# Prompt attention's masks: added by VectorE in PSUM in place of TensorE matmuls

## Chip, cores and metric

One core of one Trainium2 chip runs the whole program. The metric is device microseconds of that core, the median over runs of the same program. TensorE multiplies matrices into PSUM (eight banks of 512 fp32 columns on 128 partitions), VectorE and ScalarE read and write PSUM and SBUF, GpSimd works on SBUF, and transfers run on DMA queues that several engines issue.

## What is computed

The reference is one inference step of one decoder layer: an input projection, sparse attention (NSA) for 8 heads in 2 groups, retention for 4 heads, an output projection, and a convolutional FFN, for a prompt of 1024 tokens and 8 decode sequences of 4 tokens. The change touches prompt attention alone. For a block of 128 queries and a head it computes three softmaxes (compressed blocks, selected blocks, sliding window), masks each, and mixes the three results by gates. In the prompt all 16 blocks of 64 keys can be selected, so the selected branch is causal attention. Cut to what matters:

```python
s_c = jnp.einsum('bqgrd,bcgd->bgrqc', qg, kc) * scale          # compressed keys
m_c = (c_start + CMP_BLOCK - 1)[None, :] <= qpos[:, None]
p_c = jnp.where(m_c, jax.nn.softmax(jnp.where(m_c, s_c, NEG), axis=-1), 0.0)
...
s_s = jnp.einsum('bqgrd,bgqkld->bgrqkl', qg, ks) * scale       # selected keys
m_s = (kpos <= qpos[None, None, :, None, None])[:, :, None]
p_s = jax.nn.softmax(jnp.where(m_s, s_s, NEG)...)
...
s_w = jnp.einsum('bqgrd,bwgd->bgrqw', qg, kw.astype(F32)) * scale   # window
m_w = (dpos >= 0) & (dpos < WINDOW) & (wpos[None, :] >= 0)
p_w = jax.nn.softmax(jnp.where(m_w, s_w, NEG), axis=-1)
out = g[..., 0:1] * o_cmp + g[..., 1:2] * o_sel + g[..., 2:3] * o_win
```

NEG is -1e30, so a mask can be added to the scores: 0 where a key is seen and NEG where it isn't.

## The kernel before

The program is one stream of instructions for each engine. The framework orders them from the program's order, priorities that the code raises in places, and its own estimate of durations; an engine then works through its queue in order, each instruction waiting on semaphores for what it needs.

Prompt attention goes over query blocks `i` of 128 tokens in the order 3, 2, 7, 6, 1, 0, 5, 4. A block has four jobs: half `a` of the heads (2) by branch `br` (0: selected keys; 1: window and compressed keys). A job has a front and a back. The front (`query`, once for two jobs, then `softmax` for `y` = 0 and 1) makes the scores of two heads, one of each group `g`, and turns them into probabilities. The back (`values_of`) transposes the probabilities on TensorE, copies them out of PSUM as `pt` (two of three copies on VectorE, L1109, one on ScalarE, L1107) and multiplies them by the values. The front of the next job is interleaved with the back of this one. Beside them other work of TensorE is emitted by cost ratios: the last projection and the decode branch first, then the loading and splitting of `w_out`, then the output projection by pairs of blocks (`out_project`, L1240 to L1242). The FFN follows and takes nearly half of the run.

Scores are made in fp32r with queries split in a high and a low part: each score bank gets a matmul with each part (`mm`, L466, `PS<-kt,qt`), and in the window branch two of 64 columns more for the compressed keys (`PS<-kc,qt`). `geometry` sets how many banks a head needs (`nb`) and how wide they are (`hw`): the selected branch has one bank for blocks 0 to 3 and two for 4 to 7; the window has one for blocks 0 to 2 and two for 3 to 7. With one bank a head, `s_banks(2)` gives the two heads adjacent banks, and one maximum serves both (L1072). With two, each head has its own maximum over both banks (L1077). The exponential with the maximum as its bias and a sum follows on ScalarE (L1079), the reciprocal on VectorE (L1084), the gate and the scaling of the probabilities on GpSimd (L1085, L1091). Six banks serve scores and transposes in turn, so a bank comes free when its exponentials are done.

The masks are added by TensorE before the scores: an identity in fp32r (`idr`) times the mask opens the accumulation (`start=True`) in the columns that need one. `m192` holds the causal mask of the diagonal (128 columns) and beside it the compressed branch's mask (64 columns), which is copied in anew for each block (L1128); both lie in the tile `ma` with the identity. `mo` is the mask of the window's old edge, added in the first bank for blocks 4 to 7. It is loaded into `FIN` and cast to fp32r by VectorE (L1181). In a profile row an operand list `PS<-ma` is a mask matmul with `m192`, and `PS<-mo,ma` one with `mo`.

Of the kernel before, what the change touches and what calls it, by code (L numbers as in the profile page):

```python
# [7 lines left out]
F32 = mybir.dt.float32  # L8
F32R = mybir.dt.float32r
I32 = mybir.dt.int32  # L10
AF = mybir.ActivationFunctionType
ALU = mybir.AluOpType
# [47 lines left out]
def hymba(ctx: ExitStack, tc: tile.TileContext, A, O):  # L60
    nc = tc.nc
    V, S, G, T, D = nc.vector, nc.scalar, nc.gpsimd, nc.tensor, nc.sync
# [4 lines left out]
    def mk(pool, name, n, dt=F32, p=128):  # L67
        return pool.tile([p, n], dt, name=name)
# [23 lines left out]
    ident = pers("ident")  # L92
# [8 lines left out]
    kcv = open_pool("kcv", "left")  # L101
# [363 lines left out]
    def mm(o, a, b, start=False, stop=False):  # L465
        T.matmul(o, a, b, start=start, stop=stop, skip_group_check=True)  # L466
# [394 lines left out]
    with tc.high_priority(offset=4000):  # L861
        o, _ = SECT["IC"]
# [71 lines left out]
    o, n = SECT["QC"]  # L934
# [20 lines left out]
    lt = {}  # L955
# [9 lines left out]
                    S.dma_start(RAW[y].rearrange("p (i b c) -> p i b c", i=4, b=2)[:, :, b], src[:, 4 * y:4 * y + 4, b, 0])  # L965

    def masks():
        lt["a"] = kcv.tile([128, 352], F32R, name="ma", tag="ws1")
        lt.update(idr=lt["a"][:, 0:128], m192=lt["a"][:, 128:320])
        S.activation(lt["idr"], ident, AF.Copy)  # L970
        V.tensor_copy(lt["m192"][:, 0:128], HN[:, MC.off["mdiag"][0]:sum(MC.off["mdiag"])])

    def build(i):
# [68 lines left out]
    def softmax(i, a, br, y):  # L1042

        w0, nw, hw, nb = geometry(i, br)
        r = 2 * a + y
        q = [[QT[a][:, z + (2 * y + g) * 128:z + (2 * y + g + 1) * 128] for z in (0, 512)] for g in range(2)]
        if nb == 1:
            pair = s_banks(2)
            sb = [pair[:, g:g + 1] for g in range(2)]
        else:  # L1050
            sb = [s_banks(2) for g in range(2)]
        for b in range(nb):
            last = b == nb - 1
            old = br and i >= 4 and not last
            for g in range(2):
                if last:
                    mm(sb[g][:, b, hw - 128:hw + 64 * br], lt["idr"], lt["m192"][:, 0:128 + 64 * br], start=True)
                elif old:
                    mm(sb[g][:, b, 0:128], lt["idr"], lt["mo"], start=True)
                for z in range(2):  # L1060
                    mm(sb[g][:, b, 0:hw], q[g][z], KT[:, br, g, w0 + b * hw:w0 + (b + 1) * hw],
                       start=not last and not old and not z, stop=z == 1 and not (last and br))
                for z in range(2 if last and br else 0):
                    mm(sb[g][:, b, hw:hw + 64], q[g][z], KC[:, g], stop=z == 1)
        p = [(PSEL, PWIN)[br][2 * y + g] for g in range(2)]

        for c in (0,) if br == 0 else (2, 1):
            e = 4 * c + 2 * y
            cs = slice(0, hw) if c != 1 else slice(hw, hw + 64)
            bs = slice(0, nb) if c != 1 else slice(nb - 1, nb)  # L1070
            if nb == 1:
                V.tensor_reduce(st9[:, e:e + 2], pair[:, :, cs], AX.X, ALU.max, negate=True)  # L1072
            for g in range(2):
                src = sb[g][:, bs, cs]
                nm = st9[:, e + g:e + g + 1]
                if nb > 1:
                    V.tensor_reduce(nm, src, AX.XY, ALU.max, negate=True)  # L1077
                d = p[g][:, 640:704] if c == 1 else p[g][:, 0:nw]
                S.activation(d.rearrange("p (b c) -> p b c", b=src.shape[1]), src, AF.Exp, bias=nm, accum_out=st9[:, 12 + e + g:13 + e + g])  # L1079
        c0, n = (0, 1) if br == 0 else (1, 2)  # L1080
        su, sc = [st9.rearrange("p (z c j) -> p z c j", z=3, c=3)[:, z, c0:c0 + n, 2 * y:2 * y + 2] for z in (1, 2)]
        gv = gates[:, i].rearrange("p (g r c) -> p c r g", g=2, c=3)[:, 0:3:2, r] if br else gates[:, i].rearrange(
            "p (g r c) -> p c r g", g=2, c=3)[:, 1:2, r]
        V.reciprocal(sc, su)  # L1084
        G.tensor_tensor(sc, sc, gv, ALU.mult)  # L1085
        for g in range(2):
            parts = [(p[g][:, 0:nw], sc[:, n - 1, g:g + 1])]
            if br:
                parts.append((p[g][:, 640:704], sc[:, 0, g:g + 1]))
            for x, f in parts:  # L1090
                G.tensor_tensor(x, x, f.to_broadcast([128, x.shape[1]]), ALU.mult)  # L1091
# [77 lines left out]
    FIN = pm.tile([128, 512], F32, name="fin", tag="fin")  # L1169
    STG = pm.tile([128, 4608], F32, name="stg", tag="mix")  # L1170
    p2 = open_pool("p2", "right")
# [1 line left out]
    PT.extend(mk(p2, f"pt{i}", 512) for i in range(4))  # L1173
    PWIN.extend(mk(p2, f"pwin{i}", 704) for i in range(4))
    PSEL.extend(mk(p2, f"psel{i}", 1024) for i in (2, 3))
    lt["mo"] = mk(p2, "mo", 128, F32R)
    lt["cmpm"] = mk(p2, "cmpm", 120)
    o, _ = SECT["MC"]
    S.dma_start(FIN[:, 0:128], A["const"][:, o + 128:o + 256])
    S.dma_start(lt["cmpm"], A["const"][:, o + 256:o + 376])  # L1180
    V.tensor_copy(lt["mo"], FIN[:, 0:128])  # L1181
    del ring[:]

    def h_ap(a, z):
# [472 lines left out]
    while main_alive or todo or seen < len(finished):  # L1657
# [7 lines left out]
        if todo:  # L1665
            last = not main_alive and seen == NT
# [6 lines left out]
            a = todo.pop(0)  # L1673
# [176 lines left out]
```

## Time and profile before

| | |
|---|---|
| time, median of 3 runs | 1538.19 us (1536.69 to 1540.07) |
| time of the profiled execution | 1536.39 us |
| its span, first to last instruction | 1534.6 us |
| mean granted TensorE clock, share of full speed | 0.987 |
| TensorE matmul busy | 1478.0 us (96%), 10722 matmuls |
| VectorE busy | 970.4 us (63%), 1795 instructions |
| ScalarE busy | 658.3 us (43%), 1439 instructions |
| GpSimd busy | 615.0 us (40%), 789 instructions |

The profile is of one execution. Busy time is the union of an engine's instructions, and matmuls overlap their neighbours, so a busy TensorE may still have room. The mask matmuls of prompt attention run from 356.6 to 803.3 us of the span.

### The profile page before, as it was taken

What the parts mean: (1) busy time and instruction counts of PE and PEld (TensorE: products, weight loads), DVE (VectorE), ACT (ScalarE), POOL (GpSimd) and SP (SyncE); (2) the same over time, 40 slices, a digit from 0 to 9 for tenths busy, and PEclk for the clock granted to TensorE, in tenths of its full rate; (3) what the DMA queues carried; (4) which work ended last, traced back from release to release, by engine and by line L of the source; (5) the groups of instructions that cost most, each with busy time, mean ns of one, the idle gap of its engine ahead of it and who ended that gap; (6) DMA issues with size and microseconds to landing.
All of it is one profiled execution on the core that took longest, in us unless ns stands there. A gap on an engine that the chain in (4) does not pass through costs nothing.

```text
span 1534.6 us, 28716 instructions
## 1 busy us (share of the span) xinstructions
PE 1478.0 (96%) x10722; PEld 1299.8 (85%) x10722; DVE 970.4 (63%) x1795; ACT 658.3 (43%) x1439; POOL 615.0 (40%) x789
## 2 busy tenths in 40 slices
PE   7999999999899899999999899999999999999998
PEld 5898877777555568787868799999999999999998
DVE  6877534373566664646567878888877877644531
ACT  6464323144555644545455433333333334544330
POOL 3453312350233754445444233333333334444552
PEclk8999999999999899999999999999999999999999
DMA  7452301163421100101012235454455535887662
GB/s 266 140 174 70 83 18 47 40 194 119 152 90 56 56 28 15 35 26 42 15 33 79 81 105 176 157 176 158 155 168 174 174 110 173 282 254 227 197 201 67
DMA packets 129568, 184.54 MB, mean 120 GB/s; under 512 B 20356, under 2 KB 89092, under 8 KB 129428
## 3 DMA queue, kind: packets, MB, share of 16 engines
q1 hardware_dynamic: 122708, 173.57, 35.7%
q10 hardware_dynamic: 5232, 4.51, 1.0%
q0 software_dynamic: 1488, 4.63, 0.9%
q8 instruction: 84, 1.38, 0.4%
q14 instruction: 56, 0.46, 0.1%
HBM read 132.84 MB, written 49.82 MB: 119 GB/s over the span
## 4 chain that ended last, share of the span: by engine, by line
PE 83%; DVE 7%; issue 3%; DMA 2%; ACT 2%; POOL 2%; SPq 0%; DVEq 0%; ACTq 0%; POOLq 0%
PE PS L466 52%; PE PS L235 6%; PE PS L238 5%; PE PS L237 5%; PE PS L1103 3%; PE PS L1241 2%; PE PS L1240 2%; PE PS L1242 2%; DVE live L1077 1%; POOL pwin L1091 1%; PE PS L777 1%; DMA raw<-in_w_in 1%; PE PS L240 1%; DMA qbig<-in_w_in 0%; PE PS L685 0%
## 5 line engine op out<-in xcount | busy, mean ns | idle before, releaser
L466 PE MATMUL PS<-x,wop 128*128 128x264 f32 x3696 | 456.8, 286 | 9.5 <-ACT x L122 4.2
L466 PEld LDWEIGHTS PS<-x,wop 128*128 128x128 f32 x3696 | 454.4, 189 | 11.5 <-ACT x L122 4.6
L466 PE MATMUL PS<-h,wop 128*128 128x264 f32 x1848 | 225.6, 285 | 0.0
L466 PEld LDWEIGHTS PS<-h,wop 128*128 128x128 f32 x1848 | 225.4, 188 | 0.0
L123 POOL TENSOR_TENSOR wop<-sp,wop 128x512 fp32r<-128x512 f32 (+1 forms) x105 | 139.9, 1338 | 182.0 <-ACT wop L122 175.5
L122 ACT ACTIVATE wop<-sp 128x512 fp32r<-128x512 f32 x150 | 90.3, 608 | 203.2 <-PE PS L466 97.3
L123 POOL TENSOR_TENSOR wop<-rawf,wop 128x512 fp32r<-128x512 f32 x42 | 69.0, 1643 | 119.2 <-ACT wop L122 119.2
L1077 DVE TENSOR_REDUCE live<-PS 128x1 f32<-128x640 f32 (+5 forms) x112 | 72.0, 653 | 60.8 <-PE PS L466 47.9
L466 PE MATMUL PS<-kt,qt 128*128 128x320 f32 (+5 forms) x400 | 103.3, 354 | 7.1 <-ACT vt L1079 5.1
L1085 POOL TENSOR_TENSOR live<-live 128x2 f32<-128x2 f32 (+1 forms) x64 | 13.0, 204 | 219.7 <-DVE live L1084 187.3
L235 PE MATMUL PS<-wh,xt 128*128 128x512 f32 (+1 forms) x240 | 93.5, 391 | 7.5 <-ACT xt L122 7.5
L1109 DVE COPY pt<-PS 128x512 f32<-128x512 f32 (+1 forms) x99 | 66.8, 684 | 28.3 <-PE PS L1103 26.2
L466 PE MATMUL PS<-pt,vt 128*64 128x256 f32 x528 | 78.4, 403 | 6.1 <-DVE pt L1109 4.9
L1079 ACT ACTIVATE pwin<-PS,live 128x64 f32<-128x64 f32 (+5 forms) x128 | 61.4, 485 | 52.8 <-DVE live L1077 34.5
L1091 POOL TENSOR_TENSOR pwin<-pwin,live 128x64 f32<-128x64 f32 (+5 forms) x128 | 78.9, 648 | 2.0
L466 PEld LDWEIGHTS PS<-kt,qt 128*128 128x128 f32 x400 | 64.3, 198 | 16.9 <-ACT vt L1079 5.8
L238 PE MATMUL PS<-wh,xt 128*128 128x512 f32 (+1 forms) x192 | 75.5, 393 | 2.8 <-DVE xt L123 2.8
L1240 PE MATMUL PS<-mix,wo 128*128 128x256 f32 (+1 forms) x256 | 75.9, 297 | 1.2 <-ACT mix L122 1.1
L123 DVE TENSOR_TENSOR h<-rawf,h 128x528 fp32r<-128x528 f32 x51 | 44.1, 873 | 50.6 <-ACT h L122 50.4
L237 PE MATMUL PS<-wl,xt 128*128 128x512 f32 (+1 forms) x192 | 75.2, 393 | 0.0
L235 PE MATMUL PS<-wh,xa 128*128 128x512 f32 (+1 forms) x192 | 74.0, 386 | 1.0 <-ACT qbig L253 0.4
L1241 PE MATMUL PS<-mix,wo 128*128 128x256 f32 (+1 forms) x256 | 74.0, 289 | 0.5 <-DVE mix L123 0.5
(385 smaller groups left out, 3061.4 us busy)
## 6 DMA issues: line engine op xcount, KB each, us to landing
rawf<-in_w_ffn_in SPq DMA_DIRECT2D x30, 512.0 KB, 3.4
rawf<-scr_x SPq DMA_DIRECT2D x51, 264.0 KB, 3.5
scr_x<-rbig SPq DMA_DIRECT2D x44, 264.0 KB, 2.6
ws<-in_w_ffn_out SPq DMA_DIRECT2D x64, 176.0 KB, 3.1
scr_s<-ws SPq DMA_DIRECT2D x64, 176.0 KB, 2.1
scr_x<-qbig SPq DMA_DIRECT2D x33, 264.0 KB, 2.1
ga<-in_cache_sel SPq DMA_DIRECT2D x64, 128.0 KB, 2.1
sp<-scr_s SPq DMA_DIRECT2D x32, 256.0 KB, 3.1
```

The costliest lines, as they stand in the source:

```text
L122: a = S.activation(h, src, AF.Copy)
L123: return a.ins, (eng or V).tensor_tensor(l, src, b32(h), ALU.subtract).ins
L235: T.matmul(ps, xh(i, kk), wh[:, k], start=first, stop=False)
L237: T.matmul(ps, xh(i, kk), wl[:, k], start=False, stop=False)
L238: T.matmul(ps, xl(i, kk), wh[:, k], start=False, stop=end)
L466: T.matmul(o, a, b, start=start, stop=stop, skip_group_check=True)
L1077: V.tensor_reduce(nm, src, AX.XY, ALU.max, negate=True)
L1079: S.activation(d.rearrange("p (b c) -> p b c", b=src.shape[1]), src, AF.Exp, bias=nm, accum_out=st9[:, 12 + e + g:13 + e + g])
L1091: G.tensor_tensor(x, x, f.to_broadcast([128, x.shape[1]]), ALU.mult)
L1109: V.tensor_copy(pt[0:n], tb)
L1240: T.matmul(o, wh, MIX[:, 0, k, 0:n], start=k == 0, stop=False)
L1241: T.matmul(o, wh, MIX[:, 1, k, 0:n], start=False, stop=False)
```

## The change

The mask matmuls go. After a bank's scores are complete, VectorE adds the mask to them in PSUM, in place. Where a head has one bank, one instruction adds the mask to both heads' banks, with the mask read twice by a broadcast. Where a head has two banks, each head gets one add in its last bank and, for the window of blocks 4 to 7, one in its first. The identity copy is gone, `ma` and `mo` are plain fp32, and `mo` is loaded straight into its tile.

```diff
--- before.py
+++ after.py
@@ -965,9 +965,8 @@
                     S.dma_start(RAW[y].rearrange("p (i b c) -> p i b c", i=4, b=2)[:, :, b], src[:, 4 * y:4 * y + 4, b, 0])
 
     def masks():
-        lt["a"] = kcv.tile([128, 352], F32R, name="ma", tag="ws1")
-        lt.update(idr=lt["a"][:, 0:128], m192=lt["a"][:, 128:320])
-        S.activation(lt["idr"], ident, AF.Copy)
+        lt["a"] = kcv.tile([128, 352], F32, name="ma", tag="ws1")
+        lt.update(m192=lt["a"][:, 0:192])
         V.tensor_copy(lt["m192"][:, 0:128], HN[:, MC.off["mdiag"][0]:sum(MC.off["mdiag"])])
 
     def build(i):
@@ -1053,15 +1052,20 @@
             last = b == nb - 1
             old = br and i >= 4 and not last
             for g in range(2):
-                if last:
-                    mm(sb[g][:, b, hw - 128:hw + 64 * br], lt["idr"], lt["m192"][:, 0:128 + 64 * br], start=True)
-                elif old:
-                    mm(sb[g][:, b, 0:128], lt["idr"], lt["mo"], start=True)
                 for z in range(2):
                     mm(sb[g][:, b, 0:hw], q[g][z], KT[:, br, g, w0 + b * hw:w0 + (b + 1) * hw],
-                       start=not last and not old and not z, stop=z == 1 and not (last and br))
+                       start=not z, stop=z == 1 and not (last and br))
                 for z in range(2 if last and br else 0):
                     mm(sb[g][:, b, hw:hw + 64], q[g][z], KC[:, g], stop=z == 1)
+            ms = slice(hw - 128, hw + 64 * br)
+            m = lt["m192"][:, 0:128 + 64 * br]
+            if nb == 1:
+                V.tensor_tensor(pair[:, :, ms], pair[:, :, ms], m.unsqueeze(1).to_broadcast([128, 2, 128 + 64 * br]), ALU.add)
+            for g in range(2 if nb > 1 else 0):
+                if last:
+                    V.tensor_tensor(sb[g][:, b, ms], sb[g][:, b, ms], m, ALU.add)
+                elif old:
+                    V.tensor_tensor(sb[g][:, b, 0:128], sb[g][:, b, 0:128], lt["mo"], ALU.add)
         p = [(PSEL, PWIN)[br][2 * y + g] for g in range(2)]
 
         for c in (0,) if br == 0 else (2, 1):
@@ -1173,12 +1177,11 @@
     PT.extend(mk(p2, f"pt{i}", 512) for i in range(4))
     PWIN.extend(mk(p2, f"pwin{i}", 704) for i in range(4))
     PSEL.extend(mk(p2, f"psel{i}", 1024) for i in (2, 3))
-    lt["mo"] = mk(p2, "mo", 128, F32R)
+    lt["mo"] = mk(p2, "mo", 128)
     lt["cmpm"] = mk(p2, "cmpm", 120)
     o, _ = SECT["MC"]
-    S.dma_start(FIN[:, 0:128], A["const"][:, o + 128:o + 256])
+    S.dma_start(lt["mo"], A["const"][:, o + 128:o + 256])
     S.dma_start(lt["cmpm"], A["const"][:, o + 256:o + 376])
-    V.tensor_copy(lt["mo"], FIN[:, 0:128])
     del ring[:]
 
     def h_ap(a, z):
```

## Rows read from the trace of the kernel before

**Rows 1.** Windows of three stretches: length, then each engine's busy time and instructions.
```profile
core 0: us, PE busy (x) PEld busy (x) DVE busy (x) ACT busy (x) POOL busy (x), PEclk, DMA share, GB/s
400.00:535.00 135.00, 119.57 (x812) 78.29 (x809) 87.22 (x202) 77.01 (x224) 62.65 (x85) 0.91 0.27 88
535.00:770.00 235.00, 227.14 (x1712) 185.69 (x1711) 131.85 (x275) 113.04 (x324) 117.70 (x185) 1.00 0.09 26
770.00:835.00 65.00, 59.39 (x453) 47.56 (x450) 47.54 (x79) 33.86 (x82) 31.56 (x44) 1.00 0.18 58
```

**Rows 2.** Instructions of tile `ma`: durations in ns, first and last start.
```profile
L466 PE MATMUL PS<-ma x128: 219/327/514, 356.6 to 803.3; 128*128 128x128 f32 x64, 128*128 128x192 f32 x64
L466 PE MATMUL PS<-mo,ma x32: 222/326/330, 501.9 to 801.1; 128*128 128x128 f32 x32
...
L970 ACT ACTIVATE ma<-pers x1: 294/294/294, 14.7 to 14.7; 128x128 fp32r<-128x128 f32 x1
```

**Rows 3.** Windows of the same stretches, instructions of tile `ma` alone.
```profile
400.00:535.00 135.00, 14.46 (x43) 9.16 (x44) 0.55 (x3) 0.00 (x0) 0.91 0.27 88
535.00:770.00 235.00, 26.90 (x96) 17.72 (x96) 2.91 (x5) 0.00 (x0) 1.00 0.09 26
770.00:835.00 65.00, 5.35 (x18) 3.31 (x18) 0.00 (x0) 0.00 (x0) 1.00 0.18 58
```

**Rows 4.** Timeline of PE, two places: start, duration, instruction.
```profile
561.15 0.22 PE L466 MATMUL PS<-ma 128*128 128x128 f32 x1
561.21 0.62 PE L466 MATMUL PS<-kt,qt 128*128 128x448 f32 x2
...
703.95 0.25 PE L466 MATMUL PS<-ma 128*128 128x192 f32 x1
704.04 0.48 PE L466 MATMUL PS<-kt,qt 128*128 128x320 f32 x2
```

**Rows 5.** Chain of waits, shares by line, for the three stretches in order.
```profile
by line: PE PS L466 27.8%; PE PS L1103 9.0%; PE PS L777 6.0%; DVE live L1077 5.8%; DVE wo L123 3.7%; DMA stg<-in_w_out 3.5%; DVE qt L123 3.4%; ACT pwin L1079 3.4%; issue 3.2%; DVE live L1072 2.9%; DVE dsm L812 2.8%; ACT vt L1079 2.5%; PE PS
...
by line: PE PS L466 37.8%; PE PS L1103 15.4%; PE PS L1241 9.5%; PE PS L1240 9.5%; PE PS L1242 9.2%; issue 3.8%; DVE live L1077 1.6%; DVE rbig L1341 1.4%; DVE qbig L1341 1.3%; DVE pt L1109 1.1%; PE PS L1213 1.1%; ACT psel L1079 0.9%; POOL rb
...
by line: issue 24.8%; POOL pwin L1091 13.9%; PE PS L466 11.0%; PE PS L1241 8.9%; PE PS L1242 8.4%; PE PS L1240 8.3%; POOL vt L1091 3.8%; POOL psel L1091 3.8%; PE PS L1103 2.8%; DVE live L1077 2.7%; POOL qbig L1200 2.2%; DVE pt L1109 2.0%; P
```

**Rows 6.** VectorE adds out of PSUM, by line: min, median and max ns.
```profile
L791 DVE TENSOR_TENSOR PS<-PS,dct x4: 151/162/163, 332.9 to 470.2; 64x4 f32<-64x4 f32 x4
...
L1249 DVE TENSOR_TENSOR qbig<-PS,qbig x8: 179/180/182, 571.5 to 627.1; 128x32 f32<-128x32 f32 x8
...
L1248 DVE TENSOR_TENSOR qbig<-PS,qbig x4: 424/424/425, 571.1 to 596.3; 128x256 f32<-128x256 f32 x4
```

**Rows 7.** Windows of the three stretches, instructions of L1077 alone (VectorE).
```profile
400.00:535.00 135.00, 18.04 (x30) 0.91 0.27 88
535.00:770.00 235.00, 42.52 (x63) 1.00 0.09 26
770.00:835.00 65.00, 11.44 (x20) 1.00 0.18 58
```

**Rows 8.** Window of the first stretch, instructions of L1072 alone (VectorE).
```profile
400.00:535.00 135.00, 13.30 (x16) 0.91 0.27 88
```

**Rows 9.** Waits: PE's from 535 to 770 us, then DVE's from 350 to 840 us.
```profile
PE PS L466 <- ACT vt L1079: 2.2, 2, 1.3
PE PS L466 <- DVE pt L1109: 2.0, 3, 1.1
...
DVE live L1077 <- PE PS L466: 47.9, 40, 4.9
```

**Rows 10.** Timelines of DVE and of PE: start, duration, instruction, idle before it.
```profile
398.58 0.23 DVE L1181 CAST mo<-fin 128x128 fp32r<-128x128 f32 x1 [0.70 <-DMA fin<-in_const]
...
399.58 0.62 PE L685 MATMUL PS<-ga,qb 128*32 128x512 f32 x2 [1.02 <-DVE pdp L811]
```

**Rows 11.** The copy L1128: what its engine waited for before it (us, times).
```profile
  PE PS L466: 4.8, 4
```

**Rows 12.** Windows of 10 us, PE alone: busy time and granted clock.
```profile
520.00:530.00 10.00, 6.64 (x24) 0.55 0.42 137
530.00:540.00 10.00, 9.41 (x49) 0.77 0.18 52
```

## The prediction

> **What bounds the kernel now.** I read the windows first, cut where the work changes: 400 to 535 us (first prompt attention beside the tail of the decode branch and the loading of `w_out`), 535 to 770 us (attention beside the output projection), 770 to 835 us (the last two attention blocks and the turn to the FFN). TensorE (PE) is busy 119.6 of 135, 227.1 of 235 and 59.4 of 65 us; VectorE (DVE) 87.2, 131.9 and 47.5 us, so 65%, 56% and 73% [rows 1]. PE looks like the bound, DVE has room. Then the masks themselves: 128 matmuls read `ma` alone and 32 read `mo` with it; half of the 128 are 128 columns wide, half 192 [rows 2]. By stretch they number 43, 96 and 18, the other 3 come earlier [rows 3]. A matmul's own duration is no price, since neighbours overlap, so I read the timeline from start to next start [rows 4]. Last, the chain of waits: what of PE and of the softmax lies on the path that sets the end? In 535 to 770 the printed PE pieces alone make 82.5% (37.8 + 15.4 + 9.5 + 9.5 + 9.2 + 1.1). In 400 to 535 they make 42.8% before the line is cut, and I take 50%; there DVE, ScalarE (ACT) and a transfer fill the rest. In 770 to 835 PE has 39.4%, GpSimd (POOL) and unexplained issue time most of the rest [rows 5]. So it is a PE-bound middle between two stretches bound by latency, and the change should be worth something else in each.
>
> **What is removed from PE.** In the middle of a run of score matmuls, a mask of 128 columns holds the next one back by 0.06 us (561.15 to 561.21) and one of 192 columns by 0.09 us (703.95 to 704.04) [rows 4]. Where a mask comes first after other work its gap is longer, but the first score matmul would then take over that start, so I count the short gaps everywhere. Narrow ones: 64 + 32 = 96, times 0.06 = 5.8 us; wide ones: 64 times 0.09 = 5.8 us; 11.5 us together with rounding, 0.072 us each. The weight loads of the identity go with them and are inside these gaps. On the path: (43 + 3) x 0.072 = 3.3 us, at 50% 1.65; 96 x 0.072 = 6.9 us, at 82.5% 5.7; 18 x 0.072 = 1.3 us, at 39% 0.5. Saved: 7.85 us. The ends are 0 (PE waits for the softmax anyway) and 11.5.
>
> The Trainium skill (TensorE: Matmul & The Clock Gate, Back-to-back issue gap) gives about 81 ns for each 128-column matmul in a sustained stream of weight loads and matmuls, and 56 ns for an isolated one. By the sustained figure the narrow masks would be an estimated 7.8 us instead of 5.8 and the forecast about 1.4 us lower; the trace's 0.06 us, inside a stream, agrees with the isolated figure and not with the sustained one, and the row decides.
>
> **What is added to DVE.** Counting from the geometry: selected attention has one bank a head for blocks 0 to 3, so 4 x 4 = 16 paired adds of 2 x 128 columns; the window has it for blocks 0 to 2, so 12 paired adds of 2 x 192. With two banks a head there are single adds: 32 of 128 columns (selected, blocks 4 to 7), 40 of 192 (window, blocks 3 to 7), and 32 of 128 for the old edge (window, blocks 4 to 7). That is 132 instructions. No row shows this shape added in place, so I take a line through adds of PSUM and SBUF: 32 columns 0.180 us, 256 columns 0.424 us, so 0.145 us plus 1.09 ns a column [rows 6]. An add that also writes PSUM took 0.162 us for 4 columns, 0.013 over the line, so the target should not matter [rows 6]. Prices: 0.285 (128), 0.354 (192), 0.424 (256), 0.564 (384). Sum: 64 x 0.285 + 40 x 0.354 + 16 x 0.424 + 12 x 0.564 = 18.2 + 14.2 + 6.8 + 6.8 = 46.0 us, or 0.2875 for each matmul that goes.
>
> How much of that reaches the path? Each add sits directly before a maximum (L1077, L1072) on the same engine and chain, so I give it the share that the maxima have there. In 400 to 535 the two lines make 5.8% + 2.9% of 135 us, 11.7 us on the chain, of 18.0 + 13.3 us busy: 37%. In 535 to 770 L1077 has 1.6% of 235 us, 3.8 of 42.5: 9%. In 770 to 835, 2.7% of 65 us, 1.8 of 11.4: 15% [rows 5, 7, 8]. Adds by stretch follow the removed matmuls: 46 x 0.2875 = 13.2 us, at 37% 4.9; 96 x 0.2875 = 27.6 us, at 9% 2.5; 18 x 0.2875 = 5.2 us, at 15% 0.8. Cost: 8.2 us. The ends are 0, all of it in DVE's idle 27 to 44%, and 46.0, all on the path; the first is nearer, since PE waits little for DVE in the middle: 2.0 us for `pt` copies and 2.2 us for an exponential [rows 9].
>
> No wait of a new kind appears for most adds: the maximum already waits for the same matmuls, and the add takes its place. Two are new. The old-edge add waits for the first bank while PE still fills the second; that is early, not late. And in blocks with two banks the program names the second head's add ahead of the first head's maximum. Behind them in DVE's queue stand `pt` copies (PE waits for these before it multiplies by V) and the splits of the query.
>
> **What moves.** The old-edge mask now lands straight in its tile. Before, DVE cast it from `FIN` at 398.58 us, after 0.70 us of waiting for that transfer, and PE then waited 1.02 us for the next DVE instruction [rows 10]. The chain passes there. Waiting and cast go: 0.9 us saved. The transfer stays on ScalarE's queue with the same size; its first reader comes at 501.9 us [rows 2], so its landing is covered by 100 us. The copy of the compressed mask (L1128) waited 4.8 us in 4 places for PE to have read the old mask [rows 11]; now only DVE reads it. I take half in the first stretch, half later: 2.4 x 37% + 2.4 x 9% = 1.1 us saved, between 0 and 4.8. The identity copy on ScalarE (0.29 us at 14.7 us into the run [rows 2]) is far from anything that waits, and I cost it at nothing; if it had cover no longer it would be 0.3 us.
>
> **Sum.** -7.85 + 8.2 - 0.9 - 1.1 = about -1.7 us, against the profiled execution's 1536.4 us (span 1534.6 and 1.8 around it): 1534.7. The median of the runs shown, 1538.2, lies 1.8 above the profiled one, so the forecast as a median is 1536.5 us. That is inside 0.2% (3.1 us), about what a measurement of this kernel can tell from no change.
>
> **Rivals.**
> *PE is the bound and the adds hide.* For it: the middle stretch, where PE is busy 97% and DVE 56% [rows 1]. Then the whole 11.5 us goes, with 0.9 and 1.1 as above: -13.5, 1524.7. Against it: in the first stretch the maxima are on the chain with a 37% share. At half the shares I use for DVE it is -5.8 and already faster. Any outcome with under 15% of the adds on the path belongs here (46 x 0.15 = 6.9 against savings of 9.85).
> *DVE's queue takes PE's place (slower).* The place: a second head's add in front of the first head's maximum, and `pt` copies behind both. DVE already waited 47.9 us for score matmuls in front of L1077 [rows 9]; if the adds lengthen this everywhere as in the first stretch, 37% of 46.0 = 17.0, less 9.85, is +7.2: 1545.4. It decides from 28% on the path (46 x 0.28 = 12.9, 3 over the savings). Against it: 9% in the middle, where most adds are.
> *One more fall of the clock (slower).* In 520 to 530 us PE was busy only 6.64 of 10 and the granted clock was 0.55, and still 0.77 in the next ten: 4.5 + 2.3 = 6.8 us of full speed lost [rows 12]. Longer softmax chains could bring one more such pause: +5.1, 1543.3. Against it: in 535 to 770 the clock is 1.00 throughout [rows 1].
>
> **How the numbers follow.** Forecast, within 0.2%: 0.37; its own range is 1535.1 to 1541.3. PE bound, faster: 0.35. DVE's queue 0.20 and the clock 0.08, together slower: 0.28. The range reaches to the first rival's 1524.7, drawn in to 1526 because a full hiding in all three stretches has under 1 in 10, and on the other side past the queue's 1545.4 to 1548, where 43% of the adds would be on the path; about 2 in 10 is left out.
>
> **What would show it.** DVE busy time in 400 to 840 us about 45 us up, PE's instructions 160 fewer; paired adds near 0.42 and 0.56 us, single ones near 0.29 and 0.35. If PE is the bound, the middle shortens by 5 us or more and PE's waits for `pt` and exponentials stay as they are. If the queue decides, those waits grow and L1077 or the adds appear with twice the share on the chain. The FFN after 840 us should keep its length and only shift. I am wrong if the order of instructions changes far from the edit, if an add in PSUM costs much more than the line says, or if the first stretch gets another pause with a low clock.

## The result

The changed kernel takes 1550.58 us (median of 8 runs, 1548.01 to 1556.26) against 1540.01 for the kernel before (8 runs, 1535.92 to 1544.33): ratio 1.0087, 95% interval 1.0072 to 1.0102. These two medians lie 10.6 us apart; by the ratio it is some 13 us slower, and so it is against the 93 executions of the kernel before that ran beside the experiments (mean 1537.9 us, the change's eight 1551.3). The forecast was 1536.5, and the range ended at 1548.

The page of the changed kernel, its span and its engines' busy time (share of the span, instructions):

```profile
span 1549.2 us, 28525 instructions
...
PE 1476.3 (95%) x10562; PEld 1290.1 (83%) x10562; DVE 1006.8 (65%) x1926; ACT 657.0 (42%) x1438; POOL 614.4 (40%) x789
```

The 160 matmuls are gone, and yet PE's busy time has hardly fallen while the span grew by 14.6 us. The windows that answer to [rows 1]:

```profile
400.00:535.00 135.00, 115.37 (x751) 72.53 (x751) 91.10 (x228) 73.10 (x217) 55.84 (x78) 0.87 0.26 83
535.00:770.00 235.00, 220.79 (x1572) 176.50 (x1569) 149.82 (x344) 111.25 (x320) 120.71 (x186) 0.96 0.09 26
770.00:835.00 65.00, 54.59 (x374) 39.06 (x374) 46.20 (x97) 33.52 (x82) 28.65 (x39) 0.97 0.15 49
```

Two things moved, both against the change. PE is idle longer (235 - 220.8 = 14.2 us in the middle, 7.9 before), and the granted clock fell from 0.91, 1.00 and 1.00 to 0.87, 0.96 and 0.97. The middle is less bound by PE: in its chain of waits, which answers to the second line of [rows 5], the printed PE pieces make 70.0% in place of 82.5%, `mm` has 28.7% in place of 37.8%, and the scaling of the probabilities on POOL, which was not on the printed part, has 7.7%:

```profile
by line: PE PS L466 28.7%; PE PS L1107 12.9%; PE PS L1243 9.5%; PE PS L1245 9.5%; PE PS L1244 9.4%; issue 8.4%; POOL pwin L1095 3.8%; DVE live L1081 2.4%; POOL vt L1095 2.3%; POOL psel L1095 1.6%; DVE qt L123 1.4%; DVE pt L1113 1.1%; DVE li
```

What PE waited for from 380 to 842 us, first before, then after (us in total, times, longest). Lines moved by 4 in this part: L1103, the transposes, is L1107 after; L1091, the scaling, is L1095; L1079, the exponential, is L1083.

```profile
PE PS L466 <- ACT vt L1079: 5.3, 4, 2.9
PE PS L466 <- DVE pt L1109: 5.2, 7, 2.3
...
PE PS L1103 <- POOL pwin L1091: 1.3, 3, 0.8
...
PE PS L1103 <- ACT pwin L1079: 1.2, 4, 0.4
...
PE PS L685 <- ACT psel L1079: 0.4, 1, 0.4
```

```profile
PE PS L466 <- DVE pt L1113: 6.7, 9, 1.8
PE PS L466 <- ACT vt L1083: 5.7, 3, 3.4
PE PS L1107 <- ACT pwin L1083: 5.5, 7, 1.7
PE PS L1107 <- POOL pwin L1095: 5.0, 5, 1.5
PE PS L685 <- ACT vt L1083: 3.5, 2, 2.3
```

The transposes wait for probabilities that POOL hasn't scaled yet (5.0 us, before 1.3), and transposes and the decode branch's matmuls (L685) wait for exponentials (5.5 and 3.5 us, before 1.2 and 0.4), some of them exponentials whose result they don't read, so for the score bank that these free. Over all lines of the two views, which go down to 0.2 us, the waits that end with an exponential or a scaling of prompt attention grew from 15.7 to 28.2 us. The softmax chain is late; VectorE's `pt` copies, which I had feared for, grew by 1.5 us only.

### The account

To compare kernels I cut each one's stretch from 380 us to the start of the last attention block's final copy into windows of 10 us. *Idle* is length less PE's busy time. *Clock* is the sum over the windows of (1 - granted clock) x PE's busy time, the full-speed work lost to the lower level. *Rest* is busy time less that, PE's work at full speed. The two whole stretches, before and after:

```profile
380.00:814.40 434.40, 404.90 (x2912) 304.87 (x2910) 257.24 (x564) 222.08 (x629) 201.66 (x299) 0.97 0.16 49
```

```profile
380.00:827.90 447.90, 403.29 (x2747) 294.43 (x2745) 292.78 (x694) 220.48 (x628) 203.16 (x299) 0.94 0.15 47
```

| kernel | length | idle | clock | rest | ratio to before |
|---|---|---|---|---|---|
| before | 434.4 | 29.5 | 9.7 | 395.2 | 1 |
| the change | 447.9 | 44.6 | 25.0 | 378.3 | 1.0087 |
| the same program again (e17) | 452.7 | 43.0 | 30.5 | 379.1 | 1.0109 |
| e1 paired adds only | 446.8 | 35.1 | 22.1 | 389.6 | 1.0086 |
| e2 two-bank adds only | 444.7 | 40.4 | 19.3 | 385.0 | 1.0097 |
| e3 no masks at all | 423.9 | 32.7 | 10.0 | 381.2 | 0.9937 |
| e4 matmuls and adds | 450.8 | 36.9 | 16.3 | 397.7 | 1.0097 |
| e5 change + fillers | 451.0 | 39.5 | 17.2 | 394.3 | 1.0106 |
| e6 before + fillers | 438.3 | 22.3 | 7.0 | 409.0 | 1.0024 |
| e7 before + VectorE load | 442.0 | 32.8 | 13.7 | 395.6 | 1.0025 |
| e8 before, masks last | 434.8 | 28.6 | 10.7 | 395.6 | 0.9980 |
| e9 change, FRONT 0.40 | 439.6 | 39.2 | 17.3 | 383.1 | 1.0020 |
| e10 before, FRONT 0.40 | 436.5 | 31.1 | 9.6 | 395.8 | 1.0015 |
| e11 change, add per head | 448.0 | 45.4 | 21.4 | 381.1 | 1.0081 |
| e12 change, FRONT 0.58 | 475.0 | 50.8 | 41.3 | 382.9 | 1.0249 |
| e13 change, FRONT 0.33 | 450.2 | 45.4 | 25.1 | 379.7 | 1.0093 |
| e14 change, FRONT 0.27 | 447.2 | 45.8 | 18.8 | 382.6 | 1.0077 |
| e15 before, FRONT 0.33 | 446.2 | 33.8 | 14.4 | 398.1 | 1.0056 |
| e16 paired, FRONT 0.40 | 444.0 | 29.4 | 29.6 | 385.0 | 1.0027 |
| e18 e9 + `pt` copies moved | 444.6 | 42.8 | 17.7 | 384.0 | 1.0078 |

Each account is of one profiled execution. The change and e17, which are one program, differ by 1.6 in idle, 5.5 in clock and 0.8 in rest; e11, which has the same order too (see below), differs from the change by 0.8, 3.6 and 2.8. So single entries are good to some 3 us, the clock's to some 5. After less before: rest -16.9, idle +15.1, clock +15.3, together +13.5 of the 14.6 us by which the span grew.

The clock's part is no accident of one profile. Over its eight executions the change was granted a mean clock of 0.975 to 0.980, and over its 93 executions the kernel before 0.979 to 0.990. Time x (1 - granted clock) averages 35.3 us against 21.2, and time x granted clock 1516.0 against 1516.7. Yet 1 us of clock loss is less than 1 us of time: among the 93 executions, which are one program, time rises by 0.60 us with each us of it (95% interval 0.50 to 0.70, each session's mean taken out). At that rate the 14.1 us make an estimated 7 to 10 of the 13 us. Nor does the loss alone make a kernel slow: e16 has 12.9 us more of it than the kernel before beside it, averaged over executions, and takes 4.9 us longer.

### The profile page after: what moved, and what is told of

The parts are those of the page before. It is cut to its first block, busy times and chain, and to the rows that moved or that the text cites. A ratio compares the mean times of both kernels' runs of the same rounds, so it can differ in the third digit from the quotient of the medians.

```text
span 1549.2 us, 28525 instructions
## 1 busy us (share of the span) xinstructions
PE 1476.3 (95%) x10562; PEld 1290.1 (83%) x10562; DVE 1006.8 (65%) x1926; ACT 657.0 (42%) x1438; POOL 614.4 (40%) x789
## 4 chain that ended last, share of the span: by engine, by line
PE 76%; DVE 11%; issue 4%; DMA 3%; ACT 3%; POOL 2%; SPq 0%; DVEq 0%; ACTq 0%; POOLq 0%
PE PS L466 49%; PE PS L235 4%; PE PS L237 4%; PE PS L238 4%; PE PS L1107 4%; PE PS L1245 2%; PE PS L1244 2%; PE PS L1243 2%; DVE live L1081 1%; DMA raw<-in_w_in 1%; DVE pt L1113 1%; PE PS L777 1%; POOL pwin L1095 1%; DMA ict<-in_const 1%; PE PS L685 1%
## 5 line engine op out<-in xcount | busy, mean ns | idle before, releaser
L466 PE MATMUL PS<-kt,qt 128*128 128x320 f32 (+5 forms) x400 | 109.3, 377 | 14.6 <-ACT vt L1083 5.7
L1089 POOL TENSOR_TENSOR live<-live 128x2 f32<-128x2 f32 (+1 forms) x64 | 13.8, 216 | 224.7 <-DVE live L1088 205.2
L466 PEld LDWEIGHTS PS<-kt,qt 128*128 128x128 f32 x400 | 68.2, 207 | 41.4 <-issue 13.8
L466 PE MATMUL PS<-pt,vt 128*64 128x256 f32 x528 | 82.7, 418 | 8.0 <-DVE pt L1113 6.7
L1083 ACT ACTIVATE pwin<-PS,live 128x64 f32<-128x64 f32 (+5 forms) x128 | 61.6, 484 | 53.0 <-DVE live L1081 39.0
L1081 DVE TENSOR_REDUCE live<-PS 128x1 f32<-128x640 f32 (+5 forms) x112 | 72.2, 652 | 12.1 <-ACT pwin L1083 10.2
L1095 POOL TENSOR_TENSOR pwin<-pwin,live 128x64 f32<-128x64 f32 (+5 forms) x128 | 77.9, 640 | 2.3
```

## The experiments

Every ratio is to the kernel before on the same chip in the same session.

### Which adds cost, and which masks save

e1 keeps the adds only where a head has one bank, e2 only where it has two; elsewhere the mask matmuls stay. e3 has neither matmuls nor adds, so it leaves out the masks of prompt attention. e4 has both, so that each mask is added twice, which leaves the probabilities as they are. The edit, shortened:

```diff
-                if last:
+                if last and pe:      # mask matmul, as in the kernel before
                     mm(sb[g][:, b, hw - 128:hw + 64 * br], lt["idr"], ...)
...
-            if nb == 1:
+            if nb == 1 and dve:      # add, as in the change
```
e1: `pe = nb > 1, dve = nb == 1`; e2: the reverse; e3: neither; e4: both everywhere.

> VectorE adds the masks only where a bank holds a head (28 paired adds); two-bank blocks keep their mask matmuls. Theory A, the adds of two-bank blocks lengthen their softmax chains and TensorE waits: no slower than before, between -3 and +2 us. Theory B, the framework's new order of the queues costs the time and not the adds: the change is nearly as large for the order, so anything up to +13 us, most likely +5 or more. Theory C, TensorE pauses more because the mask matmuls no longer fill its time, and its clock falls: about a fifth of the matmuls are gone, +2 to +4 us.

Measured: 1548.99 us, ratio 1.0086 (1.0072 to 1.0101).

> The other half of the change: VectorE adds in the two-bank blocks alone (104 adds), the one-bank blocks keep their mask matmuls. Theory A: nearly all of the slowdown, +9 to +15 us against before. Theory B: no link to which half it is; anything from 0 to +13 us. Theory C: about four fifths of the matmuls gone, +8 to +11 us.

Measured: 1550.75 us, 1.0097 (1.0074 to 1.0119).

> No masks at all in prompt attention, neither matmuls nor adds (the masking is left out). Theory A: TensorE's saving without VectorE's cost, 4 to 11 us faster than before. Theory B: as slow as the change, +5 to +15 us, since the matmuls' absence moves the order just as much. Theory C: slower than before by 5 us or more, since TensorE has the fewest instructions of all.

Measured: 1526.9 us, 0.9937 (0.9920 to 0.9954).

> The mask matmuls of before and the VectorE adds together (a masked score gets the mask twice, which changes no probability). Theory A: slower than the change by TensorE's saving that is missing, +15 to +25 us against before. Theory B: between 0 and +15 us. Theory C: TensorE is as full as before, so within 4 us of before.

Measured: 1551.83 us, 1.0097 (1.0075 to 1.0119).

The saving is real: without masks the stretch loses 14.0 us of rest and 10.5 us of length, idle and clock hardly move. So is the cost of the adds: on top of the matmuls they bring about +15 us (0.0097 of 1535). But the costs don't add up. 28 paired adds cost as much as all 132, so a price per add can't be the cause. In rest e1 saves 5.6 us with 56 matmuls and e2 10.2 with 104, both near 0.10 each; both lose it again, and more, in idle and clock. No theory holds: A fails at e1 (13 us in place of -3 to +2), B at e3, which it wanted 5 to 15 us slower, C at e1 (it gave 2 to 4) and at e4 (15 us in place of 4). That is what I went on with: late softmaxes, or the clock, or the order of the stream.

### Keeping PE busy

Two filler matmuls of 256 zero columns stand behind the last scores of each softmax and add nothing to them, in the change (e5) and in the kernel before (e6).

```diff
+            for _ in range(2 if last else 0):
+                mm(OT[:, 0:256], KT[:, 0, 0, 0:128], lt["zero"]..., stop=True)
```

> The changed kernel, with two filler matmuls (256 zero columns against key weights, accumulated onto the score bank, so they add nothing to a score) behind the last scores of each of the 64 softmaxes: 128 fillers, about 15 us of TensorE work, there to keep TensorE busy in the pause that follows the scores. Clock theory (the loss is clock that falls after longer pauses): the time at the low clock between 380 and 890 us falls from 68 to 35 us or less, and the time is -8 to +2 us against the changed kernel. Queue theory (the softmax chains are longer because VectorE's queue is): low-clock time as in the change, and +10 to +15 us against it. Order theory (another order of the instructions costs the time): anything, since the order is planned anew; no claim.

Measured: 1554.05 us, 1.0106 (1.0082 to 1.0129).

> The kernel before, with the same 128 fillers, masks still matmuls. Clock theory: before has 31 us of low clock in that stretch, of which a filler can save at most a few us, so +5 to +12 us for the fillers' own work less what the clock gives back. Queue theory: +10 to +15 us, the fillers' own work. So the clock theory needs e5 less the change to be well under e6 less before; the queue theory needs them alike.

Measured: 1541.7 us, 1.0024 (1.0007 to 1.0042).

The fillers did what they were for, to a part: in the change idle fell by 5.1 and clock by 7.8 us, and the time at the lower level from 380 to 890 us (twice the sum of (1 - granted clock) x length over windows of 10 us) went from 68 to 48 us, not to 35. But they are 16.0 us of rest, and the balance is +3.1 in the change and +3.9 before (13.8 - 7.2 - 2.7). The clock theory needed a clear difference between the two; there is none. So low clock can be bought off here only at its own price, and it can't be told by this pair whether the clock causes the loss or goes along with the pauses. The queue theory's +10 to +15 failed as well, since idle and clock took back most of the fillers' work.

### VectorE's load, and the order within a bank

e7 leaves the masks on PE and gives VectorE 132 maxima of the adds' lengths from a constant tile into one that nobody reads. e8 moves the mask matmuls behind the scores.

```diff
+            for n in (...the lengths of the adds...):        # e7
+                V.tensor_reduce(lt["junk"], b32(KT[:, 0, 0, 0:n]), AX.X, ALU.max)
```

> The kernel before, masks still matmuls, and 132 maxima on VectorE of the lengths of the adds, from a constant key tile into a tile that nobody reads, each in the place where the change has its add: VectorE has the change's load, but no softmax has to wait for TensorE before such a maximum. Chain theory (an add costs because it can only start after the scores): 0 to +5 us against before. Load theory (46 us more on VectorE's queue cost the same wherever they stand): +10 to +16 us.

Measured: 1542.82 us, 1.0025 (1.0010 to 1.0040).

> The kernel before, with each mask matmul behind its scores in place of ahead of them: the same work in another order, so that the mask waits for the query as the scores do. Order theory (the time hangs on small changes of TensorE's order): more than 5 us in either direction. Chain and clock theories: 0 to +3 us, since the sum of PE's work and the length of the softmax chain are the same.

Measured: 1534.77 us, 0.9980 (0.9964 to 0.9996).

e7 isn't the experiment that I meant. The instructions of its junk tile, with their first and last start:

```profile
L1066 DVE TENSOR_REDUCE junk<-kt x132: 258/328/554, 384.8 to 495.7; 128x1 f32<-128x128 f32 x64, 128x1 f32<-128x192 f32 x40, 128x1 f32<-128x256 f32 x16, 128x1 f32<-128x384 f32 x12
```

Since nothing holds them back, all 132 ran by 496 us, where the change's adds go on past 800. So it shows only that some 45 us more on VectorE within 111 us cost 4 us, within the chain theory's claim; what the load costs where the adds stand stays untried. e8 shows that a shift in PE's order need not cost 13 us: this one gained 0.2% (3 us, just outside the 0 to +3 of the chain and clock theories), and it is the only kernel of the study with all masks that is faster than the kernel before.

### The pace of the softmaxes

`FRONT` sets within which share of the steps of one job's values the next job's scores and softmaxes are named. It stands at 0.49 in both kernels. Smaller gives a softmax more time before its probabilities are wanted.

```diff
-    FRONT = 0.49
+    FRONT = 0.40       # e9, e10; 0.58 in e12
```

> The change with the pacing constant FRONT at 0.40 in place of 0.49: the next job's scores and softmaxes are named within 40% of the steps of this job's values in place of 49%, so each softmax has more time before its probabilities are wanted. Lead theory (TensorE pauses because the longer chain delivers the probabilities late): TensorE's idle time between 380 us and the last attention copy falls from 45 to 38 us or less, and the time by 5 us or more against the change. Bank theory (TensorE pauses because a softmax with an add holds its score banks longer): no gain, since earlier scores hold the banks no shorter: -2 to +5 us against the change.

Measured: 1540.12 us, 1.0020 (1.0004 to 1.0036).

> The kernel before with FRONT at 0.40. Lead theory: 0 to +4 us against before, whose chain is shorter and needs no more lead. Bank theory: the same shift as in the change, -2 to +5 us.

Measured: 1538.07 us, 1.0015 (0.9999 to 1.0032).

> The change with FRONT at 0.58: the other direction, the softmaxes later and closer to the use of their probabilities. Lead theory: slower than the change by 5 us or more, waits for the probabilities up. Bank theory: -5 to +2 us.

Measured: 1576.03 us, 1.0249 (1.0228 to 1.0270).

A constant that touches no mask and no add takes 10 of the 13 us away, and in the other direction adds 25. At 0.40 the change and the kernel before are level (1.0020 and 1.0015). The waits of e9, same stretch as above, after the change's 5.0, 5.5 and 6.7:

```profile
PE PS L466 <- ACT vt L1083: 5.6, 3, 3.4
PE PS L1107 <- ACT pwin L1083: 4.7, 3, 3.1
PE PS L466 <- DVE pt L1113: 4.7, 9, 1.4
...
PE PS L1107 <- POOL pwin L1095: 0.7, 2, 0.4
```

The wait for late probabilities is nearly gone (0.7 us), as the lead theory had it; the waits that end with an exponential fell less, from 22.1 to 18.5 us over all lines. Idle fell to 39.2 us, short of the 38 that the theory asked for, and clock by 7.7 in this profile (by 4 over the executions: time x (1 - granted clock) averages 31.1 us in e9, 35.3 in the change).

But other runs go against late probabilities as the cause. This wait in e12, e2 and e4:

```profile
PE PS L1107 <- POOL pwin L1095: 1.8, 4, 0.5
```

```profile
PE PS L1114 <- POOL pwin L1102: 1.9, 2, 1.5
```

```profile
PE PS L1114 <- POOL pwin L1102: 2.8, 4, 1.5
```

In e12, 25 us slower than the change, the lead theory wanted more of it than the change's 5.0 us, and there is less; the account puts +16.3 us on the clock and +6.2 on idle. e2 and e4 are as slow as the change with little of it. So the pace is shown to be worth the difference; by which wait isn't.

Is it the lead in general, or one place in the queue? e11 puts each head's last-bank add directly ahead of that head's own maximum.

```diff
-                if last:
-                    V.tensor_tensor(sb[g][:, b, ms], sb[g][:, b, ms], m, ALU.add)
-                elif old:
+                if old:
...
                 if nb > 1:
+                    if c != 1:
+                        V.tensor_tensor(sb[g][:, nb - 1, ms], sb[g][:, nb - 1, ms], m, ALU.add)
                     V.tensor_reduce(nm, src, AX.XY, ALU.max, negate=True)
```

> The change with each head's last-bank add directly ahead of its own maximum, where a head has two banks: add, maximum, exponential of the first head, then of the second, in place of both adds first. The same adds, the same work on every engine; in the change the first head's chain holds both adds, here one. Queue theory (the second head's add in front of the first head's maximum is what hurts): -4 to -10 us against the change. Chain theory in general (one add in each chain is enough): -3 to +3 us.

Measured: 1549.74 us, 1.0081 (1.0062 to 1.0100).

VectorE's timeline in one window job with two banks a head (start, duration, instruction, idle before it), the change and then e11:

```profile
583.19 0.37 DVE L1066 TENSOR_TENSOR PS<-PS,ma 128x192 f32<-128x192 f32 x1 [0.29 <-PE PS L466]
583.59 0.82 DVE L1081 TENSOR_REDUCE live<-PS 128x1 f32<-128x640 f32 x1
...
586.73 0.37 DVE L1066 TENSOR_TENSOR PS<-PS,ma 128x192 f32<-128x192 f32 x1 [0.44 <-PE PS L466]
587.13 0.82 DVE L1081 TENSOR_REDUCE live<-PS 128x1 f32<-128x640 f32 x1
```

```profile
585.36 0.37 DVE L1080 TENSOR_TENSOR PS<-PS,ma 128x192 f32<-128x192 f32 x1 [0.29 <-PE PS L466]
585.76 0.82 DVE L1081 TENSOR_REDUCE live<-PS 128x1 f32<-128x640 f32 x1
...
588.89 0.37 DVE L1080 TENSOR_TENSOR PS<-PS,ma 128x192 f32<-128x192 f32 x1 [0.44 <-PE PS L466]
589.29 0.82 DVE L1081 TENSOR_REDUCE live<-PS 128x1 f32<-128x640 f32 x1
```

Both have add, maximum, add, maximum. All five engines run the same operations on the same tiles and shapes in the same sequence in the two programs (1926 of 1926 on VectorE): the framework had already put the change's adds where e11 names them. So e11 is the change measured once more, and decides between neither theory. What speaks against the queue theory is the change's own timeline: of its 72 last-bank adds in blocks with two banks, only 6 are followed by another such add before a maximum.

### Where the rest went

> The change with FRONT at 0.33, still more lead than the 0.40 that took the time from 1550 to 1540 us. If lead is all that the change lacks: another 3 to 8 us, so 1532 to 1537, waits for probabilities at nothing. If what is left at 0.40 is score banks held longer by the adds (16 us of TensorE's waits end with an exponential there): 1538 to 1545, with those waits as before or longer.

Measured (FRONT 0.33): 1553.76 us, 1.0093 (1.0067 to 1.0119).

> The change with FRONT at 0.27. Lead alone: 0 to -4 us against the one at 0.33. Banks: +3 us or more against it, since more softmaxes compete with the transposes for six banks.

Measured (FRONT 0.27): 1551.07 us, 1.0077 (1.0052 to 1.0101).

> The kernel before with FRONT at 0.33. If lead is wanted by the add alone: 0 to +5 us against before. If the pacing constant was simply off for both: -3 us or better.

Measured (before, FRONT 0.33): 1546.85 us, 1.0056 (1.0034 to 1.0078).

> Adds only where a head has one bank (28 paired adds, 13.6 us on VectorE, in place of 56 matmuls), mask matmuls elsewhere, and FRONT at 0.40; at 0.49 this cost as much as the whole change (1549 us). Lead theory: that loss goes too: 1533 to 1540 us. Order theory (any edit of the stream costs about 13 us): 1546 us or more.

Measured (e1 with FRONT 0.40): 1543.94 us, 1.0027 (1.0010 to 1.0044).

More lead than 0.40 gives the loss back, with the bank theory's sign, but 9 us above its range. The waits of e13:

```profile
PE PS L1107 <- ACT vt L1083: 7.8, 7, 2.4
...
PE PS L1107 <- ACT pwin L1083: 4.7, 5, 2.3
PE PS L1107 <- ACT psel L1083: 4.0, 2, 2.8
...
PE PS L1107 <- POOL pwin L1095: 1.5, 1, 1.5
```

Now transposes wait 7.8 + 4.7 + 4.0 = 16.5 us for exponentials to free their banks (e9: 0.9 + 4.7 + 1.3 = 6.9), and hardly for probabilities. The kernel before loses by it too (e15, 8.6 us, above its range), but some 6 us less. From 0.33 to 0.27 the change got 2.5 us faster, within the 0 to -4 of lead alone; the +3 or more by banks didn't come. e16 shows that most of the half change's loss goes with the same constant: 0.0086 became 0.0027. Its time lies between the two ranges, 4 us above the lead theory's.

e17 was meant as a point between 0.49 and 0.40; e18 moves every sixth `pt` copy from VectorE to ScalarE in e9.

```diff
-            if ctr["pt"] % 3 == 0:
+            if ctr["pt"] % 2 == 0:       # e18, with FRONT = 0.40
                 S.activation(pt[0:n], tb, AF.Copy)
```

> The change with FRONT at 0.44, between the 0.49 that it has (1550 us) and the 0.40 that gave 1540. If the time is a smooth valley with its floor near 0.40 to 0.45, where late probabilities and held banks balance: 1533 to 1542 us. If any new order of the stream draws a time of its own between 1535 and 1555: no claim, and a time above 1545 would speak for it.

Measured: 1554.65 us, 1.0109 (1.0086 to 1.0132).

> The change with FRONT at 0.40 and every second pt copy on ScalarE in place of every third, which takes about one pt copy in six off VectorE. If what is left of the loss at 0.40 is VectorE's queue (4.8 us of TensorE's waits end with a pt copy there): 1534 to 1538 us, waits for VectorE's pt copies down to 3 us or less. If it is held banks or the clock: 1538 to 1545 us, since ScalarE's exponentials, which free the banks, then stand behind more copies.

Measured: 1549.06 us, 1.0078 (1.0057 to 1.0099).

e17 is no new point. Worked out from the loop that uses it, 0.44 gives the same interleaving of steps as 0.49 in all 31 pairs of jobs, and all five engines have the change's order instruction by instruction; it is the change, measured once more. The step at 0.40 changes 6 of the 31 interleavings. So the pace moves in steps, and I can't speak of a smooth valley. e18 lost 9 us against e9 and lies above both ranges. PE's waits for VectorE's copies stayed (5.3 us, 4.7 in e9), so the edit didn't take away what it was to test, and VectorE's queue is not cleared by it. The waits that end with an exponential didn't grow either (18.5 us in both), so that ScalarE holds the banks longer isn't shown; why e18 is slower stays open.

## Why the prediction was wrong

**The step that failed.** "One more fall of the clock" was priced at +5.1 us, given 0.08, and put aside with "in 535 to 770 the clock is 1.00 throughout" [rows 1]; the sum holds nothing for it. That is a reading of a stretch whose pauses were still short, and the change lengthened them (idle in the middle 7.9 to 14.2 us). Clock took 15.3 us in the account, in all three stretches (0.87, 0.96, 0.97). That is three events like that of [rows 12], which comes to 0.45 x 6.64 + 0.23 x 9.41 = 5.2 us in the account's measure.

Without the clock the account gives -16.9 + 15.1 = -1.8 us. That this meets my net of -1.7 is chance. In the account's terms the sum said 11.5 us less rest, and 3.65 (the part of these that lay off the path) + 8.2 - 0.9 - 1.1 = 9.85 us more idle. Both came out some 5 us larger.

**The PE saving was too small.** I took gaps of 0.06 and 0.09 us from a stream [rows 4], 11.5 us in all and 7.85 on the path, 0.072 us each over both widths. In rest the removed matmuls measured 14.0 (e3) to 16.9 us (the change), 0.088 to 0.106 each; e1 and e2 give 0.10. The Trainium skill (TensorE: Matmul & The Clock Gate, Back-to-back issue gap) has about 81 ns as the sustained figure for 128 columns, which I turned down for the row's 0.06. The runs speak for a longer gap than the row's, but none of them measures 128 columns alone.

**The price of an add was right, its reach was not.** The adds by form, from 350 to 860 us (busy time, mean ns):

```profile
L1066 DVE TENSOR_TENSOR PS<-PS,ma 128x192 f32<-128x192 f32 x40 | 14.5, 361 | 17.0 <-PE PS L466 16.8
L1068 DVE TENSOR_TENSOR PS<-PS,mo 128x128 f32<-128x128 f32 x32 | 9.4, 295 | 9.1 <-PE PS L466 8.3 <-PE PS L1107 0.6
L1066 DVE TENSOR_TENSOR PS<-PS,ma 128x128 f32<-128x128 f32 x32 | 9.3, 294 | 12.9 <-PE PS L466 12.6 <-ACT vt L1083 0.2
L1063 DVE TENSOR_TENSOR PS<-PS,ma 128x384 f32<-128x384 f32 x12 | 6.8, 565 | 6.8 <-PE PS L466 6.8
L1063 DVE TENSOR_TENSOR PS<-PS,ma 128x256 f32<-128x256 f32 x16 | 6.4, 427 | 8.4 <-PE PS L466 8.3
```

46.4 us against 46.0, each size within 10 ns, so adding in place in PSUM cost no more than that over the line. VectorE's busy time in the account's stretch rose by only 292.78 - 257.24 = 35.5 us, since an add overlaps the next instruction (here a 0.42 us add is followed after 0.33):

```profile
402.78 0.42 DVE L1063 TENSOR_TENSOR PS<-PS,ma 128x256 f32<-128x256 f32 x1
403.11 0.36 DVE L1066 TENSOR_TENSOR PS<-PS,ma 128x192 f32<-128x192 f32 x1
```

But the share on the path, taken from the share that the maxima had there (37%, 9%, 15% [rows 5, 7, 8]), gave 8.2 us, and with it 9.85 of idle; idle grew by 15.1. A share of the old path holds while the path stays where it is. Before, PE hardly ever waited for scaled probabilities (1.3 us), and that said nothing of how close they came; moved later, they set PE's start (5.0 us), and POOL's scaling, absent from the printed chain of the middle before, came onto it.

**The queue rival was right in sign and wrong in place.** It said slower, 1545.4, by the second head's add before the first head's maximum and the `pt` copies behind both. The queue had the first at 6 of 72 places only, and PE's waits for VectorE's `pt` copies grew by no more than 1.5 us; e18, which was to test these, left them as they were. The waits grew at the transposes, for POOL's scaling and for banks that exponentials hold.

**"The PE is bound" rival** got most of its saving of 13.5 (e3, 10.5 us of length) and missed that the adds lengthen the chain.

**Further signs that I named.** 160 fewer PE instructions, add prices and the unchanged FFN held: of 14.6 us of span 13.5 lie ahead of the last attention copy. "The order of instructions changes far from the edit" came true, and by e9 and e12 the order is worth as much as the whole change. So did "the first stretch gets another pause with a low clock" (0.91 to 0.87).

**What is shown and what is not.** Shown: masks on PE cost 10 us of time (e3); the adds cost more than that at the pace of 0.49, and about as much at 0.40 (e9 against e10); and the loss goes with a lower granted clock. Not shown: that late probabilities are the way, since e2, e4 and e12 lose with few such waits. Not settled: why half the change costs as much as all of it (e1, e2), and what makes the clock fall more often. Idle and clock don't keep step: e16 has before's idle (29.4) and three times its clock loss (29.6), e5 spent 16.0 us on filling and won back 12.9. That the framework's new order, beyond the adds, has a part in it was not separated; the change's instructions in the order of the kernel before were not tried.

## What to carry to other kernels

Moving work off a 97% busy engine onto one with 44% idle time need not pay when the work then stands in the chain that feeds the busy engine: look at what the consumer waits for behind the lengthened chain (here the transposes behind POOL's scaling), not at the share of the old path. When a chain gets longer, set its lead anew in the same edit, and measure the kernel before at that lead as well: here the change costs 0.9% at the old pace and nothing that can be measured at the other. Give the clock a price of its own wherever a change can bring pauses, even where it now stands at 1.00. And compare the order that the queues got before believing an experiment that reorders: e11 and e17 turned out to be the change itself.

## What the runs showed of the hardware

A short pause can be followed by a loss far larger than itself. In e16 PE was busy 2.82 of 5 us from 480 to 485 us, and then almost without a gap, yet the granted clock stood at 0.50, the lower of its two levels (1.2 of 2.4 GHz), for most of the next 20 us: some 9.9 us of full speed (the sum of (1 - granted clock) x busy time over the five windows) for 2.2 us of pause. Windows of 5 us, e16:

```profile
480.00:485.00 5.00, 2.82 (x22) 1.61 (x21) 3.37 (x13) 3.24 (x15) 3.10 (x5) 0.88 0.26 79
485.00:490.00 5.00, 5.00 (x23) 3.73 (x22) 2.87 (x7) 1.90 (x10) 2.33 (x5) 0.50 0.00 0
490.00:495.00 5.00, 5.00 (x30) 3.30 (x30) 0.67 (x4) 2.42 (x9) 0.00 (x0) 0.50 0.00 0
495.00:500.00 5.00, 4.96 (x20) 1.44 (x17) 2.80 (x11) 1.36 (x4) 2.33 (x5) 0.50 0.00 0
500.00:505.00 5.00, 5.00 (x14) 2.58 (x15) 3.70 (x6) 1.37 (x3) 0.00 (x0) 0.58 0.01 3
```

The change has the like from 425 us, where a longer pause than before's is followed by three windows at 0.50:

```profile
425.00:430.00 5.00, 3.27 (x20) 2.13 (x17) 4.33 (x7) 2.67 (x8) 0.00 (x0) 0.92 0.38 105
430.00:435.00 5.00, 4.91 (x25) 2.56 (x26) 2.08 (x11) 2.99 (x13) 4.43 (x6) 0.50 0.00 0
435.00:440.00 5.00, 4.33 (x19) 3.75 (x19) 3.38 (x13) 2.43 (x8) 0.00 (x0) 0.50 0.02 5
440.00:445.00 5.00, 4.67 (x23) 2.53 (x25) 2.36 (x11) 2.41 (x12) 2.45 (x4) 0.50 0.00 0
```

In the kernel before PE was busy 3.71, 4.35 and 4.38 of 5 us from 430 to 445 us and kept a clock of 1.00 throughout. From 480 to 490 us it fell, by a little:

```profile
430.00:435.00 5.00, 3.71 (x28) 2.13 (x28) 4.14 (x11) 4.52 (x16) 1.59 (x3) 1.00 0.16 50
435.00:440.00 5.00, 4.35 (x34) 3.68 (x34) 4.06 (x15) 4.50 (x17) 2.83 (x4) 1.00 0.02 3
440.00:445.00 5.00, 4.38 (x33) 2.55 (x33) 2.59 (x10) 2.39 (x9) 3.54 (x7) 1.00 0.01 2
...
480.00:485.00 5.00, 3.69 (x24) 2.76 (x22) 2.57 (x10) 4.57 (x20) 2.02 (x5) 0.84 0.20 52
485.00:490.00 5.00, 4.68 (x38) 3.53 (x37) 1.85 (x6) 1.84 (x8) 0.75 (x2) 0.82 0.00 0
```

So two pauses of much the same size, 3.71 and 3.69 of 5 us, one without a fall and one with 3.4 us at the lower level; how long the level stays low differs from 3.4 to 20 us. Idle totals don't tell the loss; what does was not found.
